# Modulation jobs paced by step length, interleaved first down-projection tiles, and linear attention's queries on one engine

## The chip, the cores and the metric

One core of a Trainium2 chip runs the whole program. The metric is the device time of one execution in microseconds (us), from runs on the chip. All arithmetic is in float32; large products are made of three passes over split operands (below).

## What is computed

Two blocks of two layers each run over 256 tokens of width 1024. The first block mixes sparse attention, a 31-tap and a 3-tap convolution, gates the three, and ends each layer with a convolutional feed-forward. The second block also carries 256 context tokens `z`; each of its layers is a feed-forward, a token mixing (Fourier, neighbourhood attention, gated linear attention, grouped attention) and a second feed-forward, all modulated by vectors made from a conditioning vector `c`:

```python
# first block, end of each layer
u = causal_dwconv(rms_norm(x, norm2_g) @ w_up, ffn_conv_w) + ffn_conv_b
u_gate, u_val = jnp.split(u, 2, axis=-1)
x = x + (jax.nn.silu(u_gate) * u_val) @ w_down          # 2816 -> 1024
# second block, each layer
mx = jnp.split((jax.nn.silu(c) @ w_mod[l] + b_mod[l])[:, None, :], 9, axis=-1)
mz = jnp.split(jax.nn.silu(c_ctx) @ w_mod[l] + b_mod[l], 9, axis=-1)
x = x + 0.5 * mx[2] * swiglu(modulate(rms_norm_2(x), mx[0], mx[1]), w1, w3, w2)
# linear attention: S_t = diag(exp(a_t)) S_{t-1} + k_t^T v_t ; o_t = q_t S_t, forwards and backwards
```

The changed lines compute the same values; only where and when is different.

## The kernel before, in words

**Products.** Activations lie with features on the 128 partitions and tokens along the row: 256 columns in the first block, 512 (`x` and `z` side by side) in most of the second. A weight tile is 128 output features by up to eight 128-feature input tiles. `weights` (L71) loads one into a ring of four buffers `wraw` from SyncE's queue, and `split` (L66) makes its rounded high half `whi` on ScalarE and the rest `wlo` on VectorE (on GpSimd for half of them in the first block's attention). There are three buffers each of `whi` and `wlo`. `mm` (L95) then does, for each input tile, `whi` times the activation's high and low half (L100, L101), and at the end `wlo` times the high half (L103). So TensorE does three matmuls for each input tile and needs `wlo` last.

**Feed-forward.** An up step `j` of 22 makes one tile of the hidden activations: two weight tiles (48 matmuls), an activation, and the high and low half `dh`, `dl`. In the first block (`first_layer`, L595 to L620) a three-tap convolution lies between, and `dl` is made on GpSimd. A down step of eight multiplies all 22 hidden tiles with three weight chunks of 8, 7 and 7 tiles (66 matmuls) into one bank and adds the result to the residual (L622 to L634; `feed_forward`, L884 to L893, with the last one apart at L894). In the first block the three chunks of a down step follow each other, so that the third chunk of the first step reads hidden tiles 15 to 21 right after the up steps. Its matmul banks are five.

**Modulation jobs.** The products of `c` with `w_mod` are not made on TensorE. `mod_jobs` (L760) cuts them into jobs; each loads 128 rows of 1024 numbers (512 KB) into a buffer `mraw` of the same ring as the weights (L765 and L766), and VectorE multiplies it with the conditioning vector and sums the row, once for `x` and, where needed, once for `z` (L770). Jobs are issued between steps by `run_jobs` (L778), which adds a fixed rate to an accumulator at each step:

```python
K.job_rate, K.job_due = len(K.jobs) / steps, 0.0      # mod_jobs
K.job_due += K.job_rate                               # run_jobs
while K.jobs and (all_ or K.job_due >= 1.0):
    K.jobs.pop(0)()
    K.job_due -= 1.0
```

The jobs start at up step 2, so 20 up steps and some down steps share them. There are 12 in each layer of the first block (`steps` 23, all forced out at down step 4, L631), 48 in the first feed-forward of the second block, 40 in the next and 32 in the one after (`steps` 25; in the last of these only `x` is needed). The last feed-forward has none. What is left is issued before the last down tile (L896), and `mod_finish` (L785) follows.

**Linear attention.** `gla_scores` (L1097) is called three times, for a half of 256 tokens. For seven block sizes `m` from 64 to 1 and both directions `d` it makes a difference of running sums `D` (VectorE, L1131), its exponentials `E` (ScalarE, L1137 and L1138), the scaled keys `ks` (VectorE, L1141) and the scaled queries `qs` (L1144: VectorE for `d` = 0, GpSimd for `d` = 1), and small matmuls of the two (L1151 for 64 and 32, L1158 for the rest). TensorE does input projections of the layer between them.

**Order.** Each engine works through its instructions in a fixed order that is set when the program is built: by program order, with the weights' splits moved ahead (`high_priority`, L81). A buffer of a ring is handed out in order of issue, so a load waits until the load four before it has been used up.

## Time and profile before

| What | Value |
|---|---|
| Time, median of 3 runs | 2945.33 us (2944.72 to 2951.25) |
| Profiled execution | 2947.42 us, span 2945.6 us |
| TensorE busy | 2853.4 us, 97% |
| VectorE busy | 2126.6 us, 72% |
| ScalarE busy | 1325.6 us, 45% |
| GpSimd busy | 388.0 us, 13% |
| Read from memory | 443.51 MB, 151 GB/s over the span |
| Mean granted TensorE clock | 0.992 of 2.4 GHz |

How to read it: the span is from the first to the last instruction of the profiled execution. Matmuls are pipelined, so a busy TensorE can still lose time, and the pitch of its matmuls is the better measure. A wait names the instruction that stood still and what released it. PE is TensorE, PEld its weight loads, DVE VectorE, ACT ScalarE, POOL GpSimd and SP SyncE; L69 is line 69 of the kernel.

### The profile page before, as it was taken

To read this page: it belongs to the slowest core of one execution; us is meant where nothing else is said; L and a number is where in the kernel's file an instruction comes from. 1 tells how busy PE (TensorE), PEld (TensorE's weight loads), DVE (VectorE), ACT (ScalarE), POOL (GpSimd) and SP (SyncE) were. 2 spreads that over 40 slices of the span, in tenths; PEclk is the share of its full clock that TensorE was granted. 3 is DMA by queue.
4 is the path that set the end of the run, shared out by engine and by line. 5 is a ranking of instruction groups with operands and counts; after the bars stand their busy time and mean duration, and the time that the engine had idled before them with its cause. 6 is when DMAs were issued, how large, how long until landed. Compare 5 with 4: busy or idle time off the path is not lost.

```text
span 2945.6 us, 47619 instructions
## 1 busy us (share of the span) xinstructions
PE 2853.4 (97%) x18738; PEld 2557.2 (87%) x18738; DVE 2126.6 (72%) x3788; ACT 1325.6 (45%) x2189; POOL 388.0 (13%) x225
## 2 busy tenths in 40 slices
PE   7989999999899999999999899999999999999999
PEld 7889999998899999888788579888888888877999
DVE  7999789789986897777657855777645554484664
ACT  4455666544546655422225454322233322365543
POOL 3333422033234210000000300000000000010000
PEclk9999999999999999999999999999999999999999
DMA  6445556654455576555542112455534444322455
GB/s 206 144 130 162 178 183 222 215 167 138 130 160 180 180 220 215 176 183 171 166 149 95 44 52 73 158 172 169 166 109 161 161 154 142 99 80 74 160 183 152
DMA packets 127935, 447.64 MB, mean 152 GB/s; under 512 B 14304, under 2 KB 19936, under 8 KB 127072
## 3 DMA queue, kind: packets, MB, share of 16 engines
q1 hardware_dynamic: 124672, 439.14, 47.1%
q10 hardware_dynamic: 3040, 5.48, 0.5%
q8 instruction: 147, 2.41, 0.3%
q14 instruction: 76, 0.62, 0.1%
HBM read 443.51 MB, written 1.05 MB: 151 GB/s over the span
## 4 chain that ended last, share of the span: by engine, by line
PE 73%; DVE 15%; DMA 5%; issue 4%; ACT 4%; POOL 0%; SPq 0%; DVEq 0%; ACTq 0%; POOLq 0%
PE mmb L100 21%; PE mmb L101 21%; PE mmb L103 21%; DVE wlo L69 4%; DMA mraw<-in_w_mod_dram 3%; DVE mjunk L770 2%; DMA wraw<-in_w_up_dram 2%; ACT whi L68 1%; PE outb L972 1%; PE atb L939 1%; DVE opl L69 1%; PE mmb L110 1%; PE mmb L111 1%; PE mmb L109 1%; DVE uu L610 1%
## 5 line engine op out<-in xcount | busy, mean ns | idle before, releaser
L68 ACT ACTIVATE whi<-wraw 128x1024 fp32r<-128x1024 f32 (+1 forms) x688 | 714.7, 1041 | 821.6 <-PE mmb L101 624.9
L69 DVE TENSOR_TENSOR wlo<-wraw,whi 128x1024 fp32r<-128x1024 f32 (+1 forms) x575 | 699.7, 1219 | 296.3 <-ACT whi L68 192.1
L100 PE MATMUL mmb<-oph,whi 128*128 128x256 f32 x2512 | 637.1, 290 | 20.8 <-ACT whi L68 12.5
L101 PE MATMUL mmb<-opl,whi 128*128 128x256 f32 x2512 | 630.4, 288 | 5.2 <-DVE opl L69 3.0
L100 PE MATMUL mmb<-hh,whi 128*128 128x512 f32 (+1 forms) x1776 | 613.2, 357 | 1.1 <-ACT whi L68 1.1
L101 PE MATMUL mmb<-hl,whi 128*128 128x512 f32 (+1 forms) x1776 | 610.3, 356 | 0.0
L100 PEld LDWEIGHTS mmb<-oph,whi 128*128 128x128 f32 x2512 | 487.6, 194 | 35.2 <-ACT whi L68 14.7
L101 PEld LDWEIGHTS mmb<-opl,whi 128*128 128x128 f32 x2512 | 488.0, 194 | 13.3 <-DVE opl L69 4.9
L770 DVE SCALAR_TENSOR_TENSOR mjunk<-mraw,cvec 128x1024 f32<-128x1024 f32 x256 | 315.2, 1231 | 223.5 <-DMA mraw<-in_w_mod_dram 217.6
L100 PEld LDWEIGHTS mmb<-hh,whi 128*128 128x128 f32 x1776 | 337.0, 190 | 54.5 <-issue 7.4
L103 PE MATMUL mmb<-hh,wlo 128*128 128x512 f32 (+1 forms) x1776 | 379.1, 355 | 3.2 <-DVE wlo L69 3.2
L101 PEld LDWEIGHTS mmb<-hl,whi 128*128 128x128 f32 x1776 | 336.9, 190 | 48.3 <-issue 2.9
L103 PE MATMUL mmb<-oph,wlo 128*128 128x256 f32 x2512 | 357.8, 285 | 4.0 <-DVE wlo L69 4.0
L69 POOL TENSOR_TENSOR wlo<-wraw,whi 128x1024 fp32r<-128x1024 f32 x113 | 286.1, 2533 | 487.7 <-ACT whi L68 415.9
L100 PE MATMUL mmb<-dh,whi 128*128 128x256 f32 (+1 forms) x1122 | 344.6, 329 | 3.3 <-ACT dh L68 3.3
L101 PE MATMUL mmb<-dl,whi 128*128 128x256 f32 (+1 forms) x1122 | 343.7, 328 | 1.3 <-POOL dl L69 1.3
L103 PEld LDWEIGHTS mmb<-hh,wlo 128*128 128x128 f32 x1776 | 297.9, 189 | 52.5 <-DVE wlo L69 5.3
L103 PEld LDWEIGHTS mmb<-oph,wlo 128*128 128x128 f32 x2512 | 326.7, 193 | 5.8 <-DVE wlo L69 5.2
L100 PEld LDWEIGHTS mmb<-dh,whi 128*128 128x128 f32 x1122 | 214.7, 191 | 22.3 <-ACT dh L68 3.7
L101 PEld LDWEIGHTS mmb<-dl,whi 128*128 128x128 f32 x1122 | 214.6, 191 | 19.9 <-POOL dl L69 1.7
L275 DVE SCALAR_TENSOR_TENSOR cvb<-u,vec,cvb 128x256 f32<-128x256 f32 x480 | 212.6, 481 | 3.5
L103 PE MATMUL mmb<-dh,wlo 128*128 128x256 f32 (+1 forms) x1122 | 210.5, 329 | 1.3 <-DVE wlo L69 1.2
(336 smaller groups left out, 2876.4 us busy)
## 6 DMA issues: line engine op xcount, KB each, us to landing
wraw<-in_w_ff_dram SPq DMA_DIRECT2D x208, 512.0 KB, 3.6
wraw<-in_w_in_dram SPq DMA_DIRECT2D x200, 512.0 KB, 3.6
mraw<-in_w_mod_dram SPq DMA_DIRECT2D x144, 512.0 KB, 4.2
wraw<-in_w_up_dram SPq DMA_DIRECT2D x88, 512.0 KB, 4.3
wraw<-in_w_y_dram SPq DMA_DIRECT2D x64, 512.0 KB, 3.5
wraw<-in_w_ff_dram SPq DMA_DIRECT2D x64, 448.0 KB, 3.4
wraw<-in_w_down_dram SPq DMA_DIRECT2D x32, 448.0 KB, 4.0
wraw<-in_w_down_dram SPq DMA_DIRECT2D x16, 512.0 KB, 4.3
```

Source lines behind the costliest of these rows:

```text
L68: nc.scalar.activation(hi, src, AF.Copy)
L69: (lo_eng or nc.vector).tensor_tensor(lo, src, hi.bitcast(F32), op=OP.subtract)
L100: nc.tensor.matmul(ps, hi[:, k], xh[:, k0 + k], start=start and k == 0, stop=False)
L101: nc.tensor.matmul(ps, hi[:, k], xl[:, k0 + k], start=False, stop=False)
L103: nc.tensor.matmul(ps, lo[:, k], xh[:, k0 + k], start=False, stop=stop and k == kt - 1)
L109: nc.tensor.matmul(ps, hi[:, k], a, start=start, stop=False)
L110: nc.tensor.matmul(ps, hi[:, k], b, start=False, stop=False)
L111: nc.tensor.matmul(ps, lo[:, k], a, start=False, stop=stop)
L275: nc.vector.scalar_tensor_tensor(box[0], u[:, j, t:t + S], V("cw", 31 * j + t), box[0], op0=OP.mult, op1=OP.add)
L610: nc.vector.scalar_tensor_tensor(uu[:, d:], pe[:, :S - d], V("fw", 3 * t + 2 - d), uu[:, d:], op0=OP.mult, op1=OP.add)
L770: nc.vector.scalar_tensor_tensor(junk, raw, 1.0, K.cvec[:, e], op0=OP.mult, op1=OP.mult, accum_out=K.mods[l][:, e, 8 * m + k:8 * m + k + 1])
L939: nc.tensor.matmul(ps[:, :n], self.q[:, self.pair, tb * P:(tb + 1) * P], self.kpad[:, self.key(e), self.keys[0]:self.keys[1]], start=True, ...
```

## The change

`run_jobs` takes a weight for the length of a step. In the first block an up step counts 1 and a down step 4, with `steps` 40; in the second block a down step counts 2.6, with `steps` 38. In the first block's down projection the first two output tiles are interleaved: their first two chunks each come before either's third. In linear attention the scaled queries of both directions are made on VectorE.

```diff
@@ -615,20 +615,27 @@
                 K.split(dh[:, j], dl[:, j], us[0], nc.gpsimd)
                 if j == 2:
                     conditioning(K, ff, A, act)
-                    mod_jobs(K, A, 0, (0, 1, 2), True, 23, (l, 2))
+                    mod_jobs(K, A, 0, (0, 1, 2), True, 40, (l, 2))
                 run_jobs(K)
                 if l == DEPTH - 1 and NF - 1 - KD <= j < NF - 1:
                     K.sq_add(xz[:, j - NF + 1 + KD, S:], j - NF + 1 + KD, 1)
-            for j in range(KD):
-                ps = K.bank()
-                for c, (k0, kt) in enumerate(((0, 8), (8, 7), (15, 7))):
-                    w = K.weights(A["w_down"][l, j, :, k0:k0 + kt], kt)
-                    K.mm(ps[:, :S], w, dh, dl, kt=kt, k0=k0, start=c == 0, stop=c == 2)
+
+            order = [(0, 0), (0, 1), (1, 0), (1, 1), (0, 2), (1, 2)] + [(j, c) for j in range(2, KD) for c in range(3)]
+            banks = {}
+            for j, c in order:
+                if c == 0:
+                    banks[j] = K.bank()
+                ps = banks[j]
+                k0, kt = ((0, 8), (8, 7), (15, 7))[c]
+                w = K.weights(A["w_down"][l, j, :, k0:k0 + kt], kt)
+                K.mm(ps[:, :S], w, dh, dl, kt=kt, k0=k0, start=c == 0, stop=c == 2)
+                if c < 2:
+                    continue
                 nc.vector.tensor_tensor(x[:, j], x[:, j], ps[:, :S], op=OP.add)
                 if l < DEPTH - 1:
                     early(K, big, x, vec1[l + 1], "n1", j)
                 K.sq_add(x[:, j], j)
-                run_jobs(K, j == 4)
+                run_jobs(K, 4.0, j == 4)
                 if l == DEPTH - 1 and j == 5:
                     mod_finish(K, vec2[0], 0, (0, 1, 2), True)
                     modulate(K, xz, 0, 0, 1, K.rms(1), range(KD))
@@ -775,8 +782,9 @@
     K.job_rate, K.job_due = len(K.jobs) / steps, 0.0
 
 
-def run_jobs(K, all_=False):
-    K.job_due += K.job_rate
+def run_jobs(K, weight=1.0, all_=False):
+
+    K.job_due += K.job_rate * weight
     while K.jobs and (all_ or K.job_due >= 1.0):
         K.jobs.pop(0)()
         K.job_due -= 1.0
@@ -877,7 +885,7 @@
             K.split(dh[:, j], dl[:, j], th)
             if jobs and j == 2:
                 conditioning(K, ff, A, act)
-                mod_jobs(K, A, *jobs, 25)
+                mod_jobs(K, A, *jobs, 38)
             run_jobs(K)
         chunks = ((0, 8), (8, 7), (15, 7))
 
@@ -888,12 +896,12 @@
                 K.mm(ps[:, :T], w, dh, dl, kt=kt, k0=k0, start=c == 0, stop=c == 2)
             for e in range(T // S):
                 gated_add(K, x, j, ps, l, 6 * f + 2, e, after is not None)
-            run_jobs(K)
+            run_jobs(K, 2.6)
             if out is not None:
                 nc.sync.dma_start(out[:, j], x[:, j, :S])
         if after:
             j = KD - 1
-            run_jobs(K, True)
+            run_jobs(K, all_=True)
             if jobs:
                 mod_finish(K, vec[jobs[0]], *jobs)
             ws = [K.weights(A["w_ff2"][l, f, j, :, k0:k0 + kt], kt) for k0, kt in chunks]
@@ -1141,7 +1149,7 @@
             nc.vector.tensor_tensor(ko, kv, Ek, op=OP.mult)
             qs = g.tile([P, 4, P], F32, name=f"qs{d}")
             qv = qd[:].rearrange("p h (n w) -> p h n w", w=2 * m)[:, :, :, qsl]
-            (nc.gpsimd if d else nc.vector).tensor_tensor(
+            nc.vector.tensor_tensor(
                 qs[:].rearrange("p h (n w) -> p h n w", w=m), qv, Eq[:, None].to_broadcast([P, 4, n, m]), op=OP.mult)
             if m >= 32:
                 for i in range(n):
```

## Rows read from the trace of the kernel before

**Rows 1.** The page, busy time of each engine.

```profile
PE 2853.4 (97%) x18738; PEld 2557.2 (87%) x18738; DVE 2126.6 (72%) x3788; ACT 1325.6 (45%) x2189; POOL 388.0 (13%) x225
```

**Rows 2.** Stretches: window, length, then PE, PEld, DVE, ACT, POOL busy (count), clock, DMA share, GB/s.

```profile
540.80:545.50 4.70, 4.26 (x20) 4.06 (x21) 3.13 (x4) 1.80 (x2) 0.73 (x1) 0.64 0.46 149
1127.00:1132.50 5.50, 4.26 (x21) 4.07 (x22) 4.46 (x7) 2.09 (x3) 1.19 (x1) 0.69 0.62 199
545.50:599.00 53.50, 53.50 (x448) 53.50 (x447) 32.33 (x46) 26.82 (x37) 2.40 (x1) 1.00 0.69 203
1210.00:1376.00 166.00, 166.00 (x734) 137.48 (x733) 131.04 (x197) 47.89 (x59) 0.00 (x0) 1.00 0.55 179
1376.00:1432.00 56.00, 52.79 (x228) 42.07 (x227) 41.34 (x61) 15.16 (x20) 0.00 (x0) 1.00 0.55 183
1432.60:1477.00 44.40, 43.09 (x189) 34.97 (x189) 29.77 (x48) 10.82 (x16) 0.00 (x0) 1.00 0.50 153
1850.00:2050.00 200.00, 199.75 (x881) 165.47 (x882) 149.96 (x221) 64.30 (x81) 0.00 (x0) 1.00 0.54 172
1610.00:1636.00 26.00, 22.46 (x260) 14.26 (x259) 22.04 (x45) 12.68 (x36) 10.68 (x8) 1.00 0.07 22
```

**Rows 3.** Timeline of TensorE, first layer's down projection: start, us, instruction, [idle before <-releaser].

```profile
531.97 0.28 PE L100 MATMUL mmb<-dh,whi 128*128 128x256 f32 x1
...
540.82 0.39 PE L100 MATMUL mmb<-dh,whi 128*128 128x256 f32 x1 [1.85 <-ACT dh L68]
541.63 0.51 PE L101 MATMUL mmb<-dl,whi 128*128 128x256 f32 x1 [0.42 <-POOL dl L69]
```

**Rows 4.** Waits of TensorE, whole span: who <- for what: us in total, times, longest.

```profile
PE atb L1158 <- DVE ks L1141: 7.1, 12, 0.8
...
PE mmb L100 <- ACT dh L68: 3.3, 2, 1.8
...
PE atb L1151 <- DVE qs L1144: 1.7, 2, 0.9
...
PE atb L1158 <- DVE qs L1144: 1.3, 2, 0.7
```

**Rows 5.** Waits of TensorE in the two up projections, 391 to 531 and 969 to 1118 us.

```profile
PE mmb L103 <- DVE wlo L69: 1.6, 2, 1.2
...
PE mmb L103 <- DVE wlo L69: 1.8, 3, 0.9
```

**Rows 6.** The page, costliest groups: busy us, mean ns of one | idle before.

```profile
L69 DVE TENSOR_TENSOR wlo<-wraw,whi 128x1024 fp32r<-128x1024 f32 (+1 forms) x575 | 699.7, 1219 | 296.3 <-ACT whi L68 192.1
...
L770 DVE SCALAR_TENSOR_TENSOR mjunk<-mraw,cvec 128x1024 f32<-128x1024 f32 x256 | 315.2, 1231 | 223.5 <-DMA mraw<-in_w_mod_dram 217.6
```

**Rows 7.** Timeline of VectorE and SyncE, down step of the first feed-forward layer.

```profile
1473.98 0.14 DVE L770 DVE_READ_ACCUMULATOR mjunk<-mraw,cvec 128x1 f32 x1
...
1475.49 7.65 SPq L766 DMA_DIRECT2D mraw<-in_w_mod_dram  x2
...
1480.41 1.23 DVE L770 SCALAR_TENSOR_TENSOR mjunk<-mraw,cvec 128x1024 f32<-128x1024 f32 x1 [3.31 <-DMA mraw<-in_w_mod_dram]
...
1481.56 1.22 DVE L69 TENSOR_TENSOR wlo<-wraw,whi 128x1024 fp32r<-128x1024 f32 x1
...
1486.42 1.23 DVE L770 SCALAR_TENSOR_TENSOR mjunk<-mraw,cvec 128x1024 f32<-128x1024 f32 x1 [1.50 <-DMA mraw<-in_w_mod_dram]
...
1488.90 0.48 DVE L851 SCALAR_TENSOR_TENSOR xz<-mmb,mods,xz 128x256 f32<-128x256 f32 x1
```

**Rows 8.** Linear attention: timeline of GpSimd and VectorE; then line 1144, ns min/median/max.

```profile
1619.95 0.29 DVE L1141 TENSOR_TENSOR ks<-gk,E 128x128 f32<-128x128 f32 x1
...
1620.16 1.82 POOL L1144 TENSOR_TENSOR qs<-qd,E 128x512 f32<-128x512 f32 x1 [1.68 <-PE atb L1151]
...
1620.75 1.38 DVE L1141 TENSOR_TENSOR ks<-gk,E 128x128 f32<-128x128 f32 x1
...
L1144 DVE TENSOR_TENSOR qs<-qd,E x21: 675/683/1797, 1594.9 to 2629.9; 128x512 f32<-128x512 f32 x21
```

## The prediction

> **What bounds the kernel now.** I read the page's busy line first. TensorE is busy 97% of the span [rows 1], so time can only come from places where it stands still or runs slowly. The view of stretches then puts such a loss beside the work that it interrupts. With nothing in the way a 256-column matmul takes 53.5 / 448 = 0.1194 us and a 512-column one 166.0 / 734 = 0.2262 us; a stretch of 200 us in the second feed-forward layer has TensorE busy for 199.75 [rows 2]. Where matmuls take longer than that, the waits and the timelines say why, and in three places the change touches the reason:
>
> - At the start of the first block's down projection the matmuls reach the last tiles of `dh` before they are made. TensorE begins at 531.97, then sits idle 1.85 us for `dh` and 0.42 us for `dl` [rows 3]; over both layers the wait for `dh` is 3.3 us [rows 4], so 1.45 us in the second. After the wait the granted clock reads 0.64 and 0.69 for about 5 us [rows 2], a mixture of the 2.4 and 1.2 GHz levels.
> - In the up projections, and in the first feed-forward layer from 1376 us on, TensorE waits for `wlo`, the low half of a weight tile, on VectorE [rows 2, 5].
> - In linear attention TensorE waits for `ks` and `qs`: 7.1 + 1.7 + 1.3 = 10.1 us in 16 waits [rows 4].
>
> **The change, part by part.**
>
> *Interleaving.* It removes the wait and the slow stretch behind it. First layer: 1.85 + (4.70 - 20 x 0.1194) = 4.2 us; second: 1.45 + (5.50 - 21 x 0.1194) = 4.4 us; together 8.6 us [rows 2 to 4]. Does the new order reach far enough? Four chunks of 8 + 7 + 8 + 7 tiles now come ahead of the first late one: 90 matmuls x 0.1194 = 10.7 us, so the late chunk starts at 542.7 and its last `dh` tile is read some 1.4 us later, at 544.1. `dh` was there at 540.82, `dl` at 541.63 [rows 3]: 3.3 and 2.5 us to spare. Two more weight splits may now stand ahead of that tile on VectorE, 1.22 us each [rows 6], which almost uses the smaller margin; I take the whole 8.6 us, with 0 as the other end (a rival below). The weight loads are the same ones in another order, and two banks instead of one are open at once, of five.
>
> *Modulation jobs.* A job is a 512 KB load in the ring of four buffers that the weights use, and one or two VectorE passes of 1.23 us [rows 6]. Playing out the accumulator: per first-block layer 10 of 12 jobs ran in the up steps, now 5, and the first five down steps take 2, 1, 1, 1, 2. In the first feed-forward layer (48 jobs, two passes each) 38 ran in the up steps, now 25; the seven down steps take 3, 3, 4, 3, 3, 3, 4 where they took 2, 2, 2, 2, 1, 1, 0. In the next (40 jobs) the up steps go from 32 to 21 and the down steps get 2 or 3; in the third (32 jobs, one pass) 25 become 16 and the down steps get 2 or 3.
>
> What leaves the up steps: the waits for `wlo` there are 1.6 and 1.8 us in the first block [rows 5]; half the jobs leave, so half the wait, 1.7 us (ends 0 and 3.4). In the first feed-forward layer the loss is 56.0 - 228 x 0.2262 = 4.4 us up and 44.4 - 189 x 0.2262 = 1.65 us down [rows 2]. It begins only after some fifteen up steps, so it is a small lag per step that eats a cushion. With 1.26 jobs a step instead of 1.92 the lag should not arise (the layer after it, at 1.6 a step, loses nothing), and I take back all 6.1 us.
>
> What the down steps pay. A step there is 66 x 0.2262 = 14.9 us. With two jobs a step the trace shows one closed loop [rows 7]: the second job ends at 1474.1, the next job's load is issued at 1475.49 (1.4 us later), it lands and its first pass starts at 1480.41 (4.9), that pass takes 1.15, a weight's `wlo` follows (1.1) and frees the buffer for the next load, which lands 3.6 us later at 1486.42, and its two passes end when `xz` starts at 1488.90 (2.6): 14.8 us, almost a whole step, though VectorE idles 4.8 us in it. So it is the ring and the in-order queue, not VectorE's busy time, that sets how many jobs fit. Three jobs in that order need 14.8 + 2.6 = 17.4 us, four 20.0. If instead the weights' splits stand ahead of the jobs, the loads overlap and three need 1.4 + 4.9 + 3 x 2.6 = 14.1, four 16.7. The cushion: that `wlo` is done at 1482.8, while TensorE starts the next step at about 1488.9 and needs it after 16 matmuls, 3.6 us later: 9.7 us. Over seven steps the worse order lags 5 x 2.5 + 2 x 5.1 = 22.7 us, less the cushion 13; the better order nothing. The middle of the two loops lags 5 x 0.8 + 2 x 3.4 = 11, hardly more than the cushion; I take 4 us (ends 0 and 13). In the next layer, five steps of three lag at most 12.5, less 9.7: 3; I take 1. The third has half the VectorE time per job: none. In the first block one job a step needs 1.4 + 4.9 + 1.15 + 1.1 + 1.3 = 9.9 us against a step of 66 x 0.1194 = 7.9, a lag of 2 us in four steps; the cushion scaled by the step is 5: at most 3, and I take 1 us per layer. Sum of the costs: 4 + 1 + 2 = 7 us. Behind a job that waits for its load stand the splits `wlo` and the residual adds, and TensorE waits for both. The later finish of the jobs is covered: the last down tile, with no jobs, still gives them 15 us before the shifts and scales are read.
>
> *Queries on VectorE.* While GpSimd runs its 1.82 us `qs`, VectorE's next `ks` takes 1.38 us instead of 0.29 and ends at about the same time [rows 8]. Moved, GpSimd's pass is gone and VectorE does `ks` and `qs` in 0.29 + 0.68 = 0.97, 0.41 us sooner than before, at each of 21 places. TensorE waits at 16 of them: 16 x 0.41 = 6.6, and a little for a `qs` of VectorE that was itself held up, to 1.80 us [rows 8]: 7 us, with ends 3 (if the weights' splits fill the time) and 10 (all of the wait).
>
> **Sum.** 8.6 + 1.7 + 6.1 + 7.0 - 7.0 = 16.4 us. The profiled execution took 2947.42 us, of which 2945.6 is its span; it is 2.1 us above the median of the runs, and I take the gain off the median: 2945.33 - 16.4 = **2929 us**.
>
> **The rivals.**
>
> *The interleaving does not help* because the splits of two more weights go ahead of the last `dh`: TensorE then waits as before, 2929 + 8.6 = 2937.5 us. For it: VectorE is the engine that makes `dh` late. Against it: 2.5 us of margin and fewer jobs ahead. Chance 0.08.
>
> *Given back in the down steps:* the worse order everywhere costs 13 + 3 + 6 = 22 instead of 7, 2944 us. For it is the closed loop of [rows 7]; against it that no queue order of the new program is known. Chance 0.06. A load's landing already differs by 1.3 us inside that one loop [rows 7]. The Trainium skill (DMA: Bandwidth & Descriptors, Latency and other measured facts) says that the fixed cost of a load grows with the load on memory, by up to 1.8 us; by that, as an estimate, a loop of three would be 19 us and this rival would fall to the slower side, but no row here separates load from order.
>
> *Slower:* the same loop, with the cushion only half full when the down steps begin, since each late load in the ring of four delays the weight load behind it. Lags of 22.7 + 12.5 + 2 x 8 = 51 us less cushions of 4.9 + 4.9 + 2.5 + 2.5 = 15 cost 36 us, against 23.4 gained: 2945.3 + 13 = 2958 us. It decides as soon as a step's lag is over 1.5 us more than I took. Against it: the up steps carried 1.92 jobs in 11 us and lost only 4.4 us. Chance 0.06.
>
> *VectorE is too full for the queries:* it gets 21 x 0.68 = 14.3 us more, and in the stretch of the first linear attention it is busy 22.04 of 26 us [rows 2]. If the slow `ks` is not GpSimd's doing, each call of seven costs 0.8 to 4.8 us of wait instead of gaining; with 8 us for the three, 2929 + 7 + 8 = 2944 us. Against it is that `ks` and GpSimd's pass end together. Chance 0.04. The Trainium skill (Perfetto Trace Analysis, Optimizing Scalar/DVE Operations) speaks for this rival, since it would offload a saturated VectorE to GpSimd; the same section warns that the two share a read port, and the trace bears out the warning more than the advice.
>
> **How the numbers follow.** The forecast, with most stalls gone and moderate costs below, has 0.76, and its own range is 2915 to 2938: below, 8.6 + 3.4 + 6.1 + 10 with no cost gives 2917, and the runs of the kernel before spread by 2 us from profile to median; above, the costs of the worse order in the first feed-forward layer alone. A measurement of this kernel can tell about 0.2%, 5.9 us, from no change. Faster by more than that: forecast and first rival, 0.84. Within it: the two cases at 2944, 0.10. Slower: 0.06. The range 2915 to 2940 leaves out those and a tail of the forecast.
>
> **What would show it.** Right: no idle before the down projection's `dh` and a granted clock of 1.00 there; no waits for `wlo` from 1376 us on; no `ks` over 0.4 us and no `qs` on GpSimd; TensorE's waits for `ks` and `qs` under 4 us in all; down steps of the first feed-forward layer at 15 us. Wrong: TensorE waits for `wlo` of several microseconds in the down steps with VectorE idle for `mraw`; a wait for `dh` at the late chunk; waits for `qs` that grow. If the down steps are 17 us long, the price of the jobs was the error; if the time is above 2940 with those steps whole, it is the queries or the interleaving.

## The result and the profile after

The changed kernel takes **2912.88 us** (median of 4 runs, 2911.12 to 2914.45), the kernel before beside it 2945.02 (4 runs, 2944.42 to 2951.25): ratio 0.9888, interval 0.9876 to 0.9900, a gain of 32.1 us. The forecast was 2929.0, with a range of 2915 to 2940: the sign was right, the gain is about twice the 16.4 us forecast, and the time lies below the range.

The busy line of the page, which answers to [rows 1]:

```profile
PE 2845.2 (98%) x18738; PEld 2551.3 (88%) x18738; DVE 2123.3 (73%) x3809; ACT 1336.4 (46%) x2189; POOL 351.1 (12%) x204
```

The same 18738 matmuls, 33 us sooner; VectorE has 21 instructions more, GpSimd 21 fewer. The averages hardly show where that comes from. The stretches do (the columns of [rows 2]; the windows lie earlier than there, as TensorE reaches the same matmuls earlier):

```profile
528.20:536.20 8.00, 8.00 (x69) 8.00 (x68) 7.62 (x11) 3.28 (x6) 1.61 (x1) 1.00 0.61 187
536.20:544.20 8.00, 8.00 (x69) 8.00 (x69) 7.93 (x13) 3.86 (x6) 0.00 (x0) 1.00 0.82 280
544.20:597.70 53.50, 50.60 (x416) 49.79 (x415) 37.88 (x57) 25.55 (x36) 5.78 (x7) 1.00 0.72 228
1105.00:1113.00 8.00, 8.00 (x69) 8.00 (x68) 7.65 (x14) 4.99 (x9) 1.73 (x2) 1.00 0.62 190
1113.00:1121.00 8.00, 8.00 (x69) 8.00 (x68) 7.80 (x11) 1.73 (x3) 0.41 (x1) 1.00 0.80 257
1355.00:1411.00 56.00, 56.00 (x249) 46.37 (x248) 38.51 (x56) 17.63 (x21) 0.00 (x0) 1.00 0.48 154
1411.40:1455.80 44.40, 44.40 (x198) 36.76 (x197) 35.66 (x56) 11.16 (x14) 0.00 (x0) 1.00 0.64 198
1587.40:1613.40 26.00, 26.00 (x275) 16.99 (x273) 20.95 (x53) 13.14 (x36) 0.31 (x1) 1.00 0.08 26
```

Both starts of the down projection run without idle time at the full clock (before: 0.64 and 0.69). The last up steps of the first feed-forward layer now hold 249 matmuls in 56 us, where 228 stood, and three of its down steps 198 where 189 stood, with VectorE busy for 35.66 us instead of 29.77. Linear attention has TensorE busy all 26 us. Only the third line is worse than its partner: 416 matmuls where the kernel before had 448.

TensorE's waits in the whole span, the part that answers to [rows 4]; then in the first block's two up projections, answering to [rows 5]; then in the first layer's down projection:

```profile
PE atb L1127 <- DVE qd L1118: 1.6, 1, 1.6
...
PE mmb L103 <- DVE wlo L69: 0.2, 1, 0.2
```

```profile
PE mmb L100 <- DVE xz L575: 0.6, 1, 0.6
...
PE mmb L100 <- DVE xz L575: 0.9, 1, 0.9
```

```profile
PE mmb L101 <- DVE opl L212: 1.6, 1, 1.6
PE mmb L100 <- ACT whi L68: 1.1, 1, 1.1
PE mmb L103 <- DVE wlo L69: 0.2, 1, 0.2
```

No row for `ks`, `qs` or `dh` is left, and the up projections wait for no weight. What is paid stands in the third fence: 1.1 us for `whi` and 0.2 for `wlo` in the first layer's down steps (the wait for `opl`, 1.6 us at the opening of the next layer, is in the kernel before too).

Both programs issue the same 16926 large matmuls (L100, L101, L103 and L109 to L111) in the same sequence but for the interleaved chunks. So the two traces can be laid side by side: the table has how much earlier TensorE reaches the same count in the changed kernel.

| Stretch | Gain, us | Forecast |
|---|---|---|
| first 40 us, unchanged code | 1.2 | 0 |
| first layer: up | 2.6 | 0.85 |
| first layer: start of down | 4.3 | 4.2 |
| first layer: rest of down | -2.1 | -1 |
| second layer: opening and attention, unchanged code | 3.0 | 0 |
| second layer: up | 4.5 | 0.85 |
| second layer: start of down | 4.0 | 4.4 |
| second layer: rest of down | -1.0 | -1 |
| first feed-forward layer of the second block | 6.7 | 6.1 - 4 |
| the two after it | 0.0 | -1 |
| linear attention, both layers | 6.4 + 3.4 | 7.0 |
| sum | 33.0 | 16.4 |

The 3.4 us of linear attention's second layer are counted to the end of the program and hold two falls of the clock, one in each trace, that nearly cancel: the kernel before has 0.68 at 2594 to 2598 us (1.5 us more than e3 below, which has the same queries and a clock of 1.00 there), the changed kernel 0.67 at 2716.5 to 2724.9 us where the kernel before has 0.80 (1.2 us, in unchanged code behind linear attention).

### The profile page after: what moved, and what is told of

Read it like the earlier page. It is cut to its first block, busy times and chain, and to the rows that moved or that the text cites. A ratio compares the mean times of both kernels' runs of the same rounds, so it can differ in the third digit from the quotient of the medians.

```text
span 2912.4 us, 47602 instructions
## 1 busy us (share of the span) xinstructions
PE 2845.2 (98%) x18738; PEld 2551.3 (88%) x18738; DVE 2123.3 (73%) x3809; ACT 1336.4 (46%) x2189; POOL 351.1 (12%) x204
## 4 chain that ended last, share of the span: by engine, by line
PE 87%; DVE 8%; ACT 2%; DMA 1%; issue 1%; POOL 0%; SPq 0%; ACTq 0%; DVEq 0%; POOLq 0%
PE mmb L100 26%; PE mmb L101 26%; PE mmb L103 25%; DVE wlo L69 2%; PE outb L980 1%; PE atb L947 1%; ACT whi L68 1%; PE mmb L110 1%; PE mmb L111 1%; PE mmb L109 1%; DVE opl L69 1%; DVE cvb L275 1%; DMA mraw<-in_w_mod_dram 1%; PE mmb L975 1%; PE atb L182 0%
## 5 line engine op out<-in xcount | busy, mean ns | idle before, releaser
L100 PE MATMUL mmb<-oph,whi 128*128 128x256 f32 x2512 | 635.0, 290 | 20.6 <-ACT whi L68 11.9
L101 PE MATMUL mmb<-opl,whi 128*128 128x256 f32 x2512 | 629.2, 287 | 5.2 <-DVE opl L69 3.0
L100 PE MATMUL mmb<-hh,whi 128*128 128x512 f32 (+1 forms) x1776 | 612.4, 357 | 1.1 <-ACT whi L68 1.1
L101 PE MATMUL mmb<-hl,whi 128*128 128x512 f32 (+1 forms) x1776 | 609.2, 355 | 0.0
L100 PEld LDWEIGHTS mmb<-oph,whi 128*128 128x128 f32 x2512 | 486.6, 194 | 34.4 <-ACT whi L68 13.7
L101 PEld LDWEIGHTS mmb<-opl,whi 128*128 128x128 f32 x2512 | 487.0, 194 | 13.2 <-DVE opl L69 4.8
L100 PEld LDWEIGHTS mmb<-hh,whi 128*128 128x128 f32 x1776 | 336.0, 189 | 55.4 <-issue 8.0
L103 PE MATMUL mmb<-hh,wlo 128*128 128x512 f32 (+1 forms) x1776 | 379.3, 355 | 0.0
L101 PEld LDWEIGHTS mmb<-hl,whi 128*128 128x128 f32 x1776 | 335.9, 189 | 47.4 <-issue 1.9
L103 PE MATMUL mmb<-oph,wlo 128*128 128x256 f32 x2512 | 357.1, 285 | 0.0
L100 PE MATMUL mmb<-dh,whi 128*128 128x256 f32 (+1 forms) x1122 | 343.2, 328 | 1.8 <-ACT whi L68 1.7
L101 PE MATMUL mmb<-dl,whi 128*128 128x256 f32 (+1 forms) x1122 | 341.9, 327 | 0.0
L103 PEld LDWEIGHTS mmb<-hh,wlo 128*128 128x128 f32 x1776 | 297.9, 189 | 46.7 <-issue 0.4
L103 PEld LDWEIGHTS mmb<-oph,wlo 128*128 128x128 f32 x2512 | 327.5, 193 | 0.2
L100 PEld LDWEIGHTS mmb<-dh,whi 128*128 128x128 f32 x1122 | 213.2, 190 | 21.0 <-ACT whi L68 2.4
L101 PEld LDWEIGHTS mmb<-dl,whi 128*128 128x128 f32 x1122 | 213.3, 190 | 18.2
L103 PE MATMUL mmb<-dh,wlo 128*128 128x256 f32 (+1 forms) x1122 | 209.1, 327 | 0.2 <-DVE wlo L69 0.2
```

The costliest lines, as they stand in the source:

```text
L100: nc.tensor.matmul(ps, hi[:, k], xh[:, k0 + k], start=start and k == 0, stop=False)
L101: nc.tensor.matmul(ps, hi[:, k], xl[:, k0 + k], start=False, stop=False)
L103: nc.tensor.matmul(ps, lo[:, k], xh[:, k0 + k], start=False, stop=stop and k == kt - 1)
```

## The experiments

All were timed beside the kernel before, whose medians in these runs were 2944 to 2947 us.

**One part taken back.** The first kernel has the old order of the chunks, the second the old pacing in both blocks, the third GpSimd's queries again, the fourth the old pacing in the first block alone (shortened; `...` stands for what is left out):

```diff
-order = [(0, 0), (0, 1), (1, 0), (1, 1), (0, 2), (1, 2)] + [(j, c) for j in range(2, KD) for c in range(3)]
+order = [(j, c) for j in range(KD) for c in range(3)]                # e1
-mod_jobs(..., 40, (l, 2)); run_jobs(K, 4.0, j == 4)
+mod_jobs(..., 23, (l, 2)); run_jobs(K, 1.0, j == 4)                  # e2, e4
-mod_jobs(K, A, *jobs, 38); run_jobs(K, 2.6)
+mod_jobs(K, A, *jobs, 25); run_jobs(K, 1.0)                          # e2
-nc.vector.tensor_tensor(qs...)
+(nc.gpsimd if d else nc.vector).tensor_tensor(qs...)                 # e3
```

> The changed kernel with the first block's down projection back in its old order; all else as changed. In the changed kernel TensorE ran 4.3 and 4.0 us ahead at this place in the two layers and then gave back 2.1 and 1.0 us inside the down steps (0.4 + 1.1 us and 0.7 us of waits for weight splits). Theory A (the order removes the wait for dh and the slow stretch behind it, and the lost cushion brings the waits further on): the wait for dh returns, about 1.5 to 1.9 us in each layer with a granted clock near 0.65 for 5 us behind it, but the later waits for splits go; net 2 x (4.2 - 1.5) = 5 us slower, 2918. Rival B (fewer jobs in the up steps make dh early by themselves): no wait for dh returns, and the time stays at 2913.

> The changed kernel with the old pacing of the modulation jobs everywhere (first block 23 and weight 1, second block 25 and weight 1); interleaving and queries as changed. Theory A (lag and cushion: a step with too many jobs lags a little each time, and waits begin when the cushion is used up, so all of them go at a lower rate): the up projections lose 2.6 and 4.5 us again, the first feed-forward layer 6.7 us, and the 3.1 us of waits in the first block's down steps go: 10.7 us slower, 2923.6. Rival B (the waits are in proportion to the jobs): 5 to 6 us slower, 2918.5. Rival C (part of the gain in the up projections was the chance of a clock that did not fall): under 5 us slower.

> The changed kernel with the queries of the second direction back on GpSimd; all else as changed. Theory A (GpSimd's pass blocks VectorE's next ks for its whole length, which delays the chain by 0.4 to 0.6 us at each of 21 places): the slow ks of 1.38 us return, TensorE's waits for ks and qs are 8 to 11 us in all, 9.8 us slower, 2922.7. Rival B (part of the 9.8 us belongs to the scheduler's other order around the stage or to the clock): slow ks return but no more than 6 us slower, below 2919.

> The changed kernel with the old pacing in the first block alone (23 and weight 1); the second block as changed. Theory A (lag and cushion): waits for splits of 2.6 and 4.5 us return in the two up projections, 3.1 us of waits go in the down steps: 4 us slower, 2917, and the first feed-forward layer is untouched, so that the second block's pacing alone is worth the other 6.7 us of e2_old_pacing. Rival B (waits in proportion to the jobs): 1.7 us come back and 3.1 go, 1.4 us faster, 2911.5.

| Kernel | Median, us | Ratio to before | Interval |
|---|---|---|---|
| e1, old order of chunks | 2919.69 | 0.9911 | 0.9895 to 0.9927 |
| e2, old pacing | 2935.13 | 0.9957 | 0.9940 to 0.9973 |
| e3, GpSimd's queries | 2925.44 | 0.9933 | 0.9917 to 0.9950 |
| e4, old pacing in the first block | 2926.47 | 0.9934 | 0.9917 to 0.9951 |

Against 2912.88 us the old order costs 6.8 us (2.1 by the profiled executions), the old pacing 22.3, of which the first block alone has 13.6, and the old queries 12.6 (8.7 by the profiles). All four cost more than was expected of them, e2 and e4 far more (10.7 and 4 us expected). The first block's pacing, forecast at less than nothing (1.7 of gain, 2 of cost), is the largest part by these medians; in the traces 8.8 us of its 13.6 lie in the stages that the edit touches. The old order alone costs little in the trace: 1.2 and 2.9 us at the two starts, of which 3.2 are won back in the down steps behind them against the changed kernel's first trace, and the wait for `dh` returns only in the second layer (1.6 us), not in the first, as was expected of both. The three medians sum to 41.7, more than the 32.1 of all together, so some parts lean on each other or the single figures are too rough; that called for each part alone.

**One part alone,** on the kernel before: the queries, the interleaved chunks, the pacing (the hunks of the change, one at a time).

> The kernel before with only the queries of linear attention moved to VectorE. The prediction's term: 7 us (3 to 10). Theory now: moving them back cost 8.7 us by the two traces, and nothing else touches linear attention, so the part is independent of the others: 8.5 to 10 us, time 2936 us where the kernel before takes 2945. Rival (the parts interact, and the 12.6 us that moving them back cost in the timed runs holds here): 2933 us or less.

> The kernel before with only the first down tiles interleaved; pacing as before. The prediction's term: 8.6 us, 4.2 and 4.4 at the two starts, time 2937 us. Theory now: with 10 jobs in the up steps VectorE comes late to the down projection, and two more weight splits go ahead of the last dh; so the first layer gains its 4 us (matmuls of its down projection lose 0.4 instead of 4.3 us) and the second does not (it loses 5 to 6 us, with a wait for wlo or dh in place of the old one): 2.5 to 4 us in all, time 2941 to 2943 us.

> The kernel before with only the new pacing of the jobs. The prediction's terms: 1.7 + 6.1 - 7 = 0.8 us, time 2944 us. Theory now: undoing it in both blocks cost 22 us, 13.6 of them in the first block, part of which was TensorE's wait for dh with the interleaved order that the old pacing made late. Without the interleaved order both waits for dh stay, about 4 us each less what an earlier VectorE takes off them: first block 6 to 10 us, first feed-forward layer 6.5 to 8.5 us, sum 13 to 18 us, time 2927 to 2932 us.

| Kernel | Median, us | Before beside it | Ratio | Interval |
|---|---|---|---|---|
| e9, only the queries | 2936.82 | 2946.35 | 0.9958 | 0.9943 to 0.9973 |
| e10, only the interleaving | 2942.20 | 2946.35 | 0.9988 | 0.9978 to 0.9997 |
| e11, only the pacing | 2930.37 | 2946.35 | 0.9935 | 0.9918 to 0.9952 |

9.5, 4.2 and 16.0 us: 29.7 in all, so the parts nearly add up, and the price of the old queries from e3 was too high. All three times stand within what was expected. In e10 the second layer does not gain. The wait for `dh` is gone, but TensorE (first fence) waits for `wlo` inside the interleaved chunks, and VectorE (second) shows why:

```profile
1128.43 1.10 PE L103 MATMUL mmb<-dh,wlo 128*128 128x256 f32 x7 [2.52 <-DVE wlo L69]
```

```profile
1126.13 1.23 DVE L776 SCALAR_TENSOR_TENSOR mjunk<-mraw,cvec 128x1024 f32<-128x1024 f32 x1 [3.35 <-DMA mraw<-in_w_mod_dram]
1127.29 0.14 DVE L776 DVE_READ_ACCUMULATOR mjunk<-mraw,cvec 128x1 f32 x1
1127.29 1.09 DVE L69 TENSOR_TENSOR wlo<-wraw,whi 128x896 fp32r<-128x896 f32 x1
```

A job stands ahead of the split, waits 3.35 us for its load, and the weight's low half comes 2.5 us late. In e11 the second layer keeps the old wait (fence: TensorE's waits from 1107 to 1176 us), though in its first layer the wait for `dh` has shrunk from 1.85 to 0.25 us by the pacing alone:

```profile
PE mmb L100 <- ACT dh L68: 2.2, 1, 2.2
PE mmb L101 <- POOL dl L69: 0.8, 1, 0.8
```

So in the first layer either part alone takes most of that loss away, and in the second only both together do.

**How many jobs an up step of the first block bears, and how many a down step.** The changed kernel once more (e5), 8 jobs in the up steps instead of 5 (e6), none (e7), and in the second block 17 of 48 jobs in the up steps instead of 25 (e8):

```diff
-mod_jobs(..., 40, (l, 2)); run_jobs(K); run_jobs(K, 4.0, j == 4)
+mod_jobs(..., 30, (l, 2)); run_jobs(K); run_jobs(K, 2.0, j == 4)        # e6
+mod_jobs(..., 40, (l, 2)); run_jobs(K, 0.0); run_jobs(K, 8.0, j == 4)   # e7
-run_jobs(K); run_jobs(K, 2.6)
+run_jobs(K, 0.7); run_jobs(K, 3.4)                                      # e8
```

> The changed kernel once more, unedited. All theories: 2912.9 us within 3 us. The question is which of the differences to the kernel before stay: if the falls of the clock behind waits of 2 us (the opening of the second layer at about 616 us, its attention at about 785 us) are luck, the profile of this execution may show them at places where the first one did not, 1.2 to 1.5 us each; the gains in the up projections, at the starts of the down projections, in the first feed-forward layer and in linear attention stay within 0.5 us each.

> First block with 8 of 12 jobs in the up steps of each layer instead of 5 (10 in the kernel before). The old pacing there cost 13.6 us over both layers for 5 jobs more. If the cost is in proportion to the jobs moved: 3/5 of 13.6 = 8 us, so 2921 us, with waits for wlo in the up steps of both layers. If it is a backlog that only builds up above a rate (VectorE falls behind by a little in each step and a cushion hides it at first): under 2 us in the up steps, and as the down steps carry 4 jobs instead of 7, the 2 and 1 us that they gave back vanish: 2910 to 2914 us.

> First block with no job in the up steps: all 12 of a layer in five down steps of 8 us. If an up step pays for each job: a further gain in the up steps, some 5 us a layer, before the down steps pay. If nothing is left to gain there (the changed kernel's up steps show no wait for wlo): up steps as they are, within 0.5 us. In the down steps VectorE is busy 35.3 of the 40 us with 7 jobs; 5 jobs more are 12.3 us of passes, 7.6 more than the time that is free. If VectorE's busy time bounds it: 4 to 8 us a layer, so 2921 to 2929 us. If each job pays its own load's latency (the closed loop of the prediction, 9.9 us a job or 14.8 for two): 12 us a layer or more, over 2937 us.

> Second block with more of its jobs in the down steps: in the first feed-forward layer 17 of 48 in the up steps and 4 or 5 in each down step, where the changed kernel has 25 and 3 or 4. Closed loop of the prediction (a job's load waits for a job's buffer): four jobs take 16.7 to 20.0 us and the down steps become 17 to 20 us long, 15 to 35 us in the first feed-forward layer and some 5 in the next, 2930 to 2950 us. Loads issued together (latency once per step): VectorE's busy time decides, 11.9 of 14.9 us now plus one job's 2.46 = 14.4, just under a step: 2913 to 2917 us, with VectorE nearly full in those steps.

| Kernel | Median, us | Ratio | Interval |
|---|---|---|---|
| e5, changed kernel again | 2916.17 | 0.9899 | 0.9884 to 0.9914 |
| e6, 8 up and 4 down | 2918.61 | 0.9907 | 0.9892 to 0.9921 |
| e7, 0 up and 12 down | 2941.78 | 0.9984 | 0.9975 to 0.9994 |
| e8, more in the second block's down steps | 2925.84 | 0.9924 | 0.9908 to 0.9941 |

e5 is 3.3 us slower than on the first occasion, a little more than expected (the kernel before beside it is 2.0 us slower too), so times of single kernels are good to some 3 us and the smaller readings below go by the traces. Even there the same code has a spread: in six executions of the changed kernel's first block (among them those of e3, e8, e12 and e14), the first layer's 528 down matmuls took 0.0, 0.6, 0.7, 2.1, 3.8 and 4.1 us more than 0.12 us each, mostly by one wait for `whi` of 0 to 2.3 us near 570 us and a slower clock behind it.

e6 loses nothing more in the first layer's up steps and 1.4 us in the second's: up to 8 jobs the price is not in proportion; at the 10 of e4 it is 4.1 and 3.7 us. That fits a backlog that builds up behind a limit. The time of e6 lies between the two that were expected, since the first layer's down steps, with fewer jobs, lose 5.1 us, by waits for `wlo` of 0.5, 0.2 and 1.8 us and a slower clock (0.85 and 0.84 from 569 to 580 us) behind the last. VectorE's waits there (529 to 600 us) in e6, then in the changed kernel (528 to 597):

```profile
DVE mjunk L777 <- DMA mraw<-in_w_mod_dram: 11.1, 4, 4.0
```

```profile
DVE mjunk L777 <- DMA mraw<-in_w_mod_dram: 1.9, 2, 1.4
```

Four jobs, each issued alone, wait 11.1 us for their loads; seven jobs, partly in pairs, 1.9 (1.4 to 4.1 in the executions named above). e7 gains nothing more in the up steps. In the first layer's down steps it then fills VectorE, 36.27 of the first 40 us, and TensorE waits 7.9 us in three waits for `whi`, whose weight's load had to wait until a job had left its buffer. The expected 4 to 8 us a layer for VectorE's busy time were too few; the 12 us expected of the closed loop came (11.9 and 12.9 us more than in the changed kernel's first trace), but not by its mechanism, in which each job pays its load's latency: VectorE waits 0.3 us in all for the jobs' loads there (529 to 600 us).

```profile
529.40:569.40 40.00, 34.64 (x266) 34.23 (x264) 36.27 (x57) 14.18 (x23) 1.57 (x1) 0.91 0.70 224
```

e8 goes over the limit of the second block. Its first four down steps lose nothing, though the jobs come in groups of four and five; the fifth, sixth and seventh lose 0.9, 2.2 and 3.9 us (7.2 us in the layer, nothing in the next two). The first two lines are its third and fourth step, the others the fifth and the seventh; then the waits of TensorE and of SyncE's queue from 1414.7 to 1543 us:

```profile
1444.50:1459.40 14.90, 14.90 (x68) 12.33 (x67) 13.88 (x23) 3.25 (x5) 0.00 (x0) 1.00 0.64 193
1459.40:1474.60 15.20, 15.20 (x69) 12.59 (x68) 13.33 (x24) 3.36 (x5) 0.00 (x0) 1.00 0.73 226
1474.60:1490.00 15.40, 15.04 (x67) 12.13 (x65) 14.01 (x23) 4.15 (x7) 0.00 (x0) 1.00 0.71 223
...
1505.00:1520.00 15.00, 13.12 (x51) 10.38 (x50) 13.36 (x22) 3.77 (x5) 0.00 (x0) 0.89 0.71 211
```

```profile
PE mmb L100 <- ACT whi L68: 4.6, 3, 2.0
```

```profile
SPq L75 <- DVE mjunk L777: 27.3, 13, 2.6
```

The third step, with 13.88 us of VectorE's work, loses nothing, and the seventh, with 13.36, most: VectorE's busy time alone does not say which step pays. TensorE waits for `whi`; ScalarE, which makes it, waits 50.4 us in 15 waits for the weights' loads in this stretch (never in the changed kernel from 1411.4 to 1540 us); and SyncE holds these loads back until a job's pass has freed a buffer of the ring (second fence; 9.0 us in 7 waits in the changed kernel). The 7.2 us are less than the 15 to 35 us expected of the closed loop and more than the 0 to 4 of the rival. They are part of the 9.7 us by which e8 is slower than e5; the first block's code is the same in both.

**Are jobs cheaper together?** e6 suggests that grouped loads share one latency. e13 is e6 with its four down jobs in two pairs; e14 is the changed kernel with the second block's down jobs one by one behind each weight chunk, at the same rate:

```diff
-run_jobs(K, 2.0, j == 4)
+run_jobs(K, 5.0 if j == 0 else 0.0, j == 2)     # e13, against e6
                 K.mm(ps[:, :T], w, dh, dl, kt=kt, k0=k0, start=c == 0, stop=c == 2)
+                run_jobs(K, 2.6 / 3)             # e14
-            run_jobs(K, 2.6)
```

> The earlier kernel with 8 of 12 jobs in the up steps of the first block (2918.6 us), but its four down jobs issued as two pairs, behind the first and the third down step, instead of one by one. With single jobs the first layer's down steps lost 5.1 us of matmul pitch, and VectorE stood 11.1 us in four waits for the jobs' loads, with weight splits behind it. If each wait is a load's latency paid singly: two waits instead of four, about 5 us of waiting, and the first layer's loss falls to 2.5 us or less, time 2914 to 2916 us. If it is the number of jobs that counts, whatever their grouping: 2918 to 2919 us.

> The changed kernel with as many jobs in the second block's down steps, but issued one by one behind each weight chunk (a third of the weight each) instead of three or four together behind the step. If the prediction's worse order is what single jobs give (each pays its load's latency in the closed loop; 17.4 us for a step of three, 20 for one of four): the first feed-forward layer's down steps lose 13 to 23 us, the next layer's 3 to 12: 2928 to 2947 us, with TensorE waiting for wlo or whi and VectorE waiting for mraw 25 us or more between 1411 and 1520 us, against 12.3 in the changed kernel. If VectorE's busy time decides (11.9 of 14.9 us a step either way) or the ring's other buffers keep enough loads in flight: 2913 to 2917 us, and the grouping does not matter.

e13: 2916.51 us, ratio 0.9900 (0.9879 to 0.9921). VectorE's wait for the loads falls from 11.1 to 3.2 us in the first layer and from 5.2 to 0.7 in the second, as expected of grouping. The matmuls' loss falls from 5.1 to 3.2, not to 2.5, within the spread given above, and the times of e5, e6 and e13 can't be told apart: whether the shorter wait is worth anything to the end stays open. e14: 2915.03 us, 0.9900 (0.9881 to 0.9919): single jobs in the second block cost nothing. Its stretches for three down steps, VectorE's waits from 1411.4 to 1516 us, and the same row of the changed kernel:

```profile
1411.80:1426.70 14.90, 14.90 (x68) 12.33 (x67) 11.03 (x18) 3.49 (x4) 0.00 (x0) 1.00 0.61 195
1426.70:1441.60 14.90, 14.90 (x68) 12.33 (x67) 12.63 (x21) 3.72 (x5) 0.00 (x0) 1.00 0.64 206
1441.60:1456.50 14.90, 14.90 (x67) 12.37 (x66) 12.00 (x19) 3.73 (x6) 0.00 (x0) 1.00 0.66 205
```

```profile
DVE mjunk L777 <- DMA mraw<-in_w_mod_dram: 17.3, 16, 2.1
```

```profile
DVE mjunk L777 <- DMA mraw<-in_w_mod_dram: 12.3, 8, 2.6
```

Twice as many waits, of 1.1 us each instead of 1.5, and VectorE has the 3 us a step to spare for them. They are not free of effect: the time from the end of the split `wlo` of a step's first weight tile to the first matmul that reads it falls from 12.5 to 6.8 us over the seven steps of e14, where it is 11.0 to 11.7 in all seven of the changed kernel. No time is lost because that lead is not used up.

**GpSimd beside VectorE.** The changed kernel, with the queries of one direction made once more on GpSimd, into a tile that nothing reads:

```diff
+for o in (0, 2) if d else ():
+    spare = g.tile([P, 2, P], F32, name="spare")
+    nc.gpsimd.tensor_tensor(spare..., qv[:, o:o + 2], Eq[:, None].to_broadcast([P, 2, n, m]), op=OP.mult)
 nc.vector.tensor_tensor(qs...)
```

> The changed kernel, with the multiplication of the queries of one direction done once more on GpSimd beside VectorE's own (in two halves, into a spare tile that nothing reads). No engine waits for the spare tile. If GpSimd's pass slows VectorE's ks beside it (the prediction's reading: 1.38 us instead of 0.29): 21 of VectorE's passes grow by up to 1.1 us each, TensorE waits for ks and qs again, and most of what moving the queries back to GpSimd cost comes back, 6 to 10 us: 2919 to 2926 us. If it was only that TensorE had to wait for GpSimd's own 1.82 us pass: 2913 us within 3 us, and ks stays at 0.3 us.

2925.83 us, ratio 0.9925 (0.9908 to 0.9941). The page's groups for `qs` and `ks` (busy us, mean ns of one) in e12, then in the changed kernel:

```profile
L1156 DVE TENSOR_TENSOR qs<-qd,E 128x512 f32<-128x512 f32 x42 | 34.7, 827 | 0.8 <-ACT E L1145 0.6
...
L1149 DVE TENSOR_TENSOR ks<-gk,E 128x128 f32<-128x128 f32 x42 | 20.6, 510 | 1.0 <-ACT E L1146 0.5 <-issue 0.2
```

```profile
L1152 DVE TENSOR_TENSOR qs<-qd,E 128x512 f32<-128x512 f32 x42 | 28.8, 686 | 0.8 <-ACT E L1145 0.6
L1149 DVE TENSOR_TENSOR ks<-gk,E 128x128 f32<-128x128 f32 x42 | 11.1, 285 | 1.6 <-ACT E L1146 0.9 <-issue 0.2
```

TensorE's row count waits again for VectorE (`qs` 3.5 us in 11 waits, `ks` 1.5 in 6), and linear attention takes 7.0 and 1.3 us longer than in the changed kernel, 8.3 in all; with GpSimd's queries in use (e3) it was 8.0. No matmul waits for the spare tile (one weight load, behind a `memset` of `qd` that stands in GpSimd's queue after it, is put down to it with 2.2 us, but TensorE comes only 0.3 us later there than in the changed kernel). So it is the work beside VectorE that costs, not the waiting for GpSimd's result. The rest of the 13 us is in the first 620 us, where this program is the changed one.

## Why the prediction was right and wrong

**Right: the interleaving's size at its place, in part by luck.** 4.2 + 4.4 us were forecast, 4.3 + 4.0 came, with the clock at 1.00. But the two parts share this gain: with the new pacing the old order loses only 1.2 and 2.9 us there (e1), and the pacing alone takes away 3.1 of the 4.3 us in the first layer (e11). The forecast counted "fewer jobs ahead" as a reason against the first rival and was right to, but it did not see that the term therefore belongs to both parts: alone, the interleaving is worth 4.2 us. With the jobs at the old rate the place gains nothing in the second layer of e10, as in that rival, though in another way: a job that waits for its load stands ahead of a split, and the wait for `dh` is gone.

**Wrong: "half the jobs leave, so half the wait, 1.7 us (ends 0 and 3.4)".** The two up projections gained 2.6 + 4.5 = 7.1 us. Two errors. The loss was under-read: beside the 3.4 us for `wlo` [rows 5] there was a wait of 0.8 us for `whi`, and of the 2.9 us left some 2.0 lay in 23 single matmuls that came 0.04 to 0.14 us late without a wait of their own. And it was taken as proportional. All of the loss left, not half, and e6 shows none at 8 jobs in the first layer either. The upper end of 3.4 us was no bound, as it rested on one kind of wait. That VectorE was nearly full does not explain it: it was busy for 92 and 93% of these stretches in the kernel before (first two lines) and for 91 and 93% in the changed one (last two), where 10 passes of jobs in place of 19 stand in each and other work, in part for later steps, fills most of the time. What is gone is the waiting, and the busy share does not show that. The prediction had used the reasoning of a lag for the first feed-forward layer ("a small lag per step that eats a cushion") and got its 6.1 us there nearly right: 6.7.

```profile
391.00:531.00 140.00, 137.76 (x1132) 136.39 (x1131) 128.95 (x220) 90.01 (x150) 24.00 (x20) 1.00 0.66 212
978.00:1118.00 140.00, 136.47 (x1113) 134.47 (x1113) 129.85 (x222) 89.49 (x153) 25.14 (x20) 1.00 0.66 209
...
389.00:528.00 139.00, 138.37 (x1146) 137.71 (x1145) 126.27 (x209) 95.85 (x156) 26.79 (x22) 1.00 0.65 206
967.00:1105.00 138.00, 137.12 (x1134) 136.39 (x1134) 128.99 (x231) 96.87 (x169) 24.28 (x21) 1.00 0.65 202
```

**Wrong: "Three jobs in that order need 14.8 + 2.6 = 17.4 us, four 20.0".** That price was the source of the 7 us of costs, of which 3.1 came, all in the first block, where the same code costs 0.0 to 4.1 us from one execution to the next. In the changed kernel the seven down steps of the first feed-forward layer, with three and four jobs each, took 15.0 us each. Nor do single jobs, the nearest to the prediction's worse order, cost so much: in e14 the lead falls by 5.7 us in seven steps, where the prediction had a lag of 22.7.

The loop of [rows 7] was read in a place where VectorE was late, and taken for one where it was ahead. Its `wlo` that is done at 1482.8 is not that of the next step, with a cushion of 9.7 us: TensorE had begun its step at 1479.47 and reads this tile at 1483.10, 0.3 us after it was made (first fence, TensorE of the kernel before). In the first five down steps of that layer in the kernel before this lead is 0.3 to 1.1 us. In the changed kernel (second fence, VectorE) a step's first `wlo` is done at 1448.85, while its step begins at 1456.25. So the cushion that the prediction subtracted was about right for the new program, by luck, and the price per job was not.

```profile
1479.47 0.39 PE L100 MATMUL mmb<-dh,whi 128*128 128x512 f32 x1
...
1483.10 1.98 PE L103 MATMUL mmb<-dh,wlo 128*128 128x512 f32 x8
```

```profile
1447.63 1.22 DVE L69 TENSOR_TENSOR wlo<-wraw,whi 128x1024 fp32r<-128x1024 f32 x1
```

VectorE's waits in the kernel before, 1432.6 to 1537 us, show the same change of state. The second line below, where it stands still until TensorE has used up an older `wlo`, begins at 1513 us (third line), when one job a step or none is left; before that it never waits for TensorE, and nearly all of its waiting is for the jobs' loads. Why the ring, when late, does not get ahead with two jobs a step, and when ahead keeps its lead with three and four, no run here separates.

```profile
DVE mjunk L770 <- DMA mraw<-in_w_mod_dram: 28.2, 10, 4.2
DVE wlo L69 <- PE mmb L103: 15.0, 5, 3.7
```

```profile
1515.09 1.23 DVE L69 TENSOR_TENSOR wlo<-wraw,whi 128x1024 fp32r<-128x1024 f32 x1 [1.60 <-PE mmb L103]
```

The quoted price rests on "So it is the ring and the in-order queue, not VectorE's busy time, that sets how many jobs fit". The runs do not refute that as the path: where too many jobs stand in the down steps (e7 and e8), the loss comes through weights' loads that wait in the queue for a buffer held by a job. But a buffer is held until VectorE's passes are done, and in these stretches VectorE is busy 83 to 93% of the time, so the two are not separated. The latency of each job's load, the largest item of the loop, is not what e7 pays (0.3 us of waiting). SyncE's queue in the changed kernel shows how the program groups the loads, three in 6 us (the second number is the time over which they are issued):

```profile
1440.22 4.71 SPq L75 DMA_DIRECT2D wraw<-in_w_ff_dram  x3
1447.80 6.21 SPq L773 DMA_DIRECT2D mraw<-in_w_mod_dram  x3
```

**Too small: the queries, 7.0 us.** The two traces give 9.8, e9 alone 9.5 (its traces: 9.7). The mechanism is the one forecast, and e12 shows it by itself. The mis-sized step is "16 x 0.41 = 6.6": it compared one `ks` and `qs` pair with the one before. The passes stand in one chain on VectorE, and all of it got shorter: `ks` fell to at most 293 ns, no `qs` takes 1.8 us any more, and even with 21 passes more VectorE spends 11.1 + 28.8 = 39.9 us on the two instead of 28.2 + 17.6 = 45.8. TensorE's 10.1 us of waits went entirely, the upper end. The Trainium skill (Perfetto Trace Analysis, Optimizing Scalar/DVE Operations) says that offloading some work of a saturated VectorE to GpSimd may make sense, and warns that it might not help, as the two share a read port. At this place e12 bears out the warning: `ks` takes 510 ns with GpSimd at work beside it and 285 without; that it is the port, no run shows.

```profile
L1149 DVE TENSOR_TENSOR ks<-gk,E x42: 270/285/293, 1572.3 to 2598.9; 128x128 f32<-128x128 f32 x42
```

**Not foreseen: 4.2 us in code that did not change.** 1.2 us in the first 40 us and 3.0 in the second layer's opening and attention are falls of the clock that happened in one execution and not in the other (last section). They are not the change's doing, and the runs' medians can be expected to hold such falls on both sides. Without them the traces give 28.8 us, beside 29.7 from the three parts alone and 32.1 from the timed runs. Whether the last 2 to 3 us are an interaction or the spread of the runs stays open; a median of four runs of the changed kernel moved by 3.3 us between two occasions (2912.88 and 2916.17).

**In sum:** the error of 16.6 us between forecast and traces is 5.4 from the up projections, 3.9 from costs that were not paid, 2.8 from the queries, 4.2 from the clock, and 0.3 from the rest (0.6 more in the feed-forward layer, 0.3 less at the two starts). The range failed at its lower end because its terms were bounded by waits that the profile lists, and taken to be independent; by how little it failed is chance, as the median of e5, the same kernel, would have lain inside.

## What to carry to other kernels

A cycle time read from a trace holds for the state in which it was read. Before charging a price per item, follow one item to the instruction that reads it, and see how far ahead the producing engine is: here the lead was 0.3 us where the loop was read and 11 us where it was to be used. The sum of the listed waits is no upper bound of what relieving an engine can gain (4.2 us listed in the up projections, 7.1 gained), and a busy share of nine tenths does not tell an engine that is late from one that is in time. And a small operation that is moved to a second engine is not free for the first when both work at the same time; measure it with a copy whose result nobody reads.

## What was not expected of the hardware

**The clock after the same wait.** At the opening of the first block's second layer TensorE waits 2.0 us for `th` in every trace. In the kernel before, the granted clock then reads 0.59 for 4 us; in the changed kernel's first trace it stays at 1.00, and in its second trace, the same program (e5), it reads 0.64 and 0.75. Matmuls run at 0.21 instead of 0.12 us in such a stretch, so 2.4 GHz gives way to 1.2, and it costs 1.5 us. Stretches of the three, in this order:

```profile
617.00:621.00 4.00, 4.00 (x23) 4.00 (x23) 3.87 (x12) 2.01 (x3) 2.38 (x1) 0.59 0.47 135
```

```profile
610.00:614.00 4.00, 3.93 (x32) 3.94 (x33) 3.87 (x10) 3.02 (x6) 2.35 (x1) 1.00 0.45 135
```

```profile
608.00:610.00 2.00, 1.63 (x8) 1.63 (x9) 2.00 (x5) 1.88 (x4) 0.05 (x1) 0.64 0.00 0
610.00:614.00 4.00, 4.00 (x28) 4.00 (x28) 3.49 (x10) 1.45 (x2) 2.34 (x1) 0.75 0.63 162
```

Such places, three or four in the first 830 us, one near 2565 and one near 2720 us, come and go between executions of the same code by 1 to 2 us each.

**Fewer jobs, longer wait.** VectorE waited 11.1 us for four loads issued alone (e6) and 3.2 us for the same four in pairs (e13); in the second layer 5.2 and 0.7 us.
